# Re-timing two kinds of background DMA around the first down projection of a Macaron layer

## The chip, the cores and the metric

One Trainium2 chip, one of its cores. The metric is device time of one launch in microseconds (us), lower is better; a kernel's time is the median of several runs. A profile is one more execution, recorded by the hardware profiler.

## The reference

One encoder layer over 512 tokens of width 1024, all float32:

```python
x = x + 0.5 * swiglu_ffn(rmsnorm(x, g1), w_gate1, w_up1, w_down1)
x = x + hybrid_mixer(rmsnorm(x, g2), ...)      # attention heads and pooling heads, one output projection
x = x + 0.5 * swiglu_ffn(rmsnorm(x, g3), w_gate2, w_up2, w_down2)
x = rmsnorm(x, g_final)

def swiglu_ffn(x, w_gate, w_up, w_down):       # 1024 -> 2816 -> 1024
    return (silu(x @ w_gate) * (x @ w_up)) @ w_down
```

Only the first feed-forward block (FFN) is touched by the change: its up projection (w_gate, w_up), its down projection (w_down), and the residual x that the down projection is added to.

## The kernel before, in words

**Products.** The 2816 features are 22 tiles of 128. Every matrix product is made of three matmuls of split parts (a high and a low part of each operand, lines 187 to 189, `mm3`). A weight block is loaded from DRAM into a `raw` buffer by the SP queue, then ScalarE (ACT) casts its high part (L131) and VectorE (DVE) subtracts to get the low part (L132); the pair lies in `parts`, or in a `whi`/`wlo` pair. TensorE (PE) works on the pair.

**Up projection, `ffn_up`.** The first five tiles of `down1.order` are "plain" (`PLAIN[0] = 5`), with full products of 512 tokens: the first two together, then n = 2, 3 and 4. The other 17 tiles are done by a seven-product block scheme (as Strassen's) in half-size products of 256 tokens, in a loop written out by hand. Each of those tiles needs two DMAs of 512 KB from `wA` (`fetch`, L458 and L459), issued two tiles ahead as soon as the buffer of an old tile is free. In each tile ACT runs, in order, a copy of one accumulator (L560), the cast of the next tile's first block (`high11`, L466, which needs the DMA of L459), then the copy of the other accumulator `a` (L560). PE may write to a copied accumulator again two products later.

**Down projection, class `Down`.** Also the seven-product scheme: T1 to T4 are sums of blocks of w_down, B11 to B22 the plain blocks. The 48 steps that make T1 to T4 (four sums, six groups g of two feature tiles, a copying and an adding step each) are DMAs from DRAM to DRAM, issued on POOL's queue (L706: `wsum<-in_wB_dram` and, where a finished sum is copied, `wsum<-wsum`; called "sums" below). An adding step waits for the step that wrote its target, a copy of a sum waits until that sum is complete. `make_sums` issues a share of them each time it is called: it first has POOL copy one element of a tile just computed (`mark`, L704), which ties the share to that point of the program, and then issues the DMAs between two entries of `bounds`. It is called once after each of the three plain tiles n = 2, 3, 4, once in each of the 17 half-size tiles, and then at the head of each product as long as shares are left. Before, `bounds` cuts the 48 steps into 22 nearly equal shares of 2 or 3: 20 in the up projection, 2 in the first two products.

**The order of the products.** `product` is called 42 times; PE takes about 2.7 us for a full one (the sixth group is half as large). Products 1 to 18 are T2, B11 and T1 for g = 0 to 5; the weights of the first six are loaded ahead at the end of the up projection (L733). From 19 on T3 and B22 alternate, then come B21 and T4. The SP queue is in program order (`manual_schedule`), so a DMA put into `down1.then[n]` is issued just behind the weight load (L759) of product n, and everything behind it in the queue waits for it to be issued. A weight load waits until its `raw` buffer is free: there are four, and so SP runs a few products ahead of PE.

**The residual.** The buffers of x (four pairs, 256 KB for each of the eight k) are used for other data during the up projection, so x is loaded again from `xT` (L814). `down1.then[8 + k]` puts one reload behind each of products 8 to 15. x[4] to x[7] are first used on DVE after product 19 (`gain(i, 1, 1, ...)`, L821), x[0] and x[1] after product 25 (`shared(i, 0, 1, ...)`, L879), x[2] and x[3] after the last T3 and B22 product, 30. Small constants follow at product 17, and the loading, filling (DVE, L245) and storing of a table for the attention bias at 18, 20 and 25.

Of the kernel before, what the change touches and what calls it, by code (L numbers as in the profile page):

```python
# [19 lines left out]
KD = D // P  # L20
NT = S // P
FF = 2816
KF = FF // P
KH = KF // 2
# [31 lines left out]
def layer(  # L56
# [31 lines left out]
    nc = tc.nc  # L88
# [12 lines left out]
    def name(what):  # L101
        n_tiles[0] += 1
        return f"{what}_{n_tiles[0]}"

    def temp(dtype=F32):
        return tpool.tile([P, S], dtype, tag="t", name=name("t"))
# [15 lines left out]
    def piece(n=1):  # L122
        for _ in range(min(n, len(todo))):
            what, *args = todo.pop(0)
            what(*args)
# [71 lines left out]
    def residual_tiles():  # L197
        pairs = [xpool.tile([P, 2 * S], F32, tag=f"x{k}", name=name("x")) for k in range(KD // 2)]
        x_pairs[:] = pairs
        return [pairs[k // 2][:, k % 2 * S : (k % 2 + 1) * S] for k in range(KD)]  # L200

    x = residual_tiles()
# [33 lines left out]
    def extended():  # L236

        flat = EXT - REL
        ext, far = temp(), temp()

        def load():
            nc.sync.dma_start(ext[:NH, :REL], rel)

        def fill():
            nc.vector.tensor_copy(far[:NH, :flat], ext[:NH, 0:1].to_broadcast([NH, flat]))  # L245

        def store():
            nc.sync.dma_start(ext_d[:, flat:], ext[:NH, :REL])
            nc.sync.dma_start(ext_d[:, :flat], far[:NH, :flat])

        return load, fill, store
# [31 lines left out]
    class Norm:  # L283


        def __init__(self, which):
            self.which, self.h, self.acc = which, {}, None
# [357 lines left out]
    class Down:  # L645
# [11 lines left out]

        def __init__(self, order, pair, block, by_token, ahead=0):  # L660

            self.order, self.pair, self.block, self.by_token = order, pair, block, by_token

            self.terms = {T1: (B11, B12), T2: (T1, B22), T3: (B12, B22), T4: (T2, B21)}
            self.wsum = {
                (i, g): dram.tile(list(block(B11, g).shape), F32, name=name("wsum"))
                for i in self.terms for g in range(G)
            }

            self.ahead = [(i, g) for g in range(2) for i in (T2, B11, T1)]  # L670
            self.loaded, self.then, self.made = {}, {}, []
            self.steps = sorted(
                (g + at + 2 * (i - T1), at, i, g)
                for i in self.terms for g in range(G) for at in range(2)
            )
            n = len(self.steps)
            self.n_sums, self.bounds = 0, [n // 2 * i // ahead for i in range(ahead)]
            left = KF - 2 if ahead else KF
            self.bounds += [n // 2 * bool(ahead) + (n - n // 2 * bool(ahead)) * i // left for i in range(left + 1)]

        def open(self, gs):

# [134 lines left out]
    def whole(make):  # L817
        return [[(make(), 0, S)] for _ in range(2)]

    def scaled(dst, acc, scale, other, op=ALU.add):  # L820
        nc.vector.scalar_tensor_tensor(dst, acc, scale, other, op0=ALU.mult, op1=op)  # L821

    def halved(acc):
        z = [temp() for _ in range(2)]
        for tt in range(2):
            nc.scalar.activation(z[tt], acc[tt][0][0], AF.Copy, scale=0.5)
        return z
# [18 lines left out]

    KPS = (2, 3, 0, 1)
    order1 = [0, 1, KH, KH + 1] + [f + KH * j for f in range(2, KH) for j in range(2)]
    down1 = Down(order1, lambda f: (f % KH, f // KH), block1, False)
    down2 = Down(list(range(KF)), lambda f: (f // 2, f % 2), block2, True, EARLY)  # L850

    with tc.tile_pool(name="act1", bufs=1, reuse_waits="tile") as apool, ExitStack() as in_order:
        down1.begin(apool)
        ffn_up(n1, wA1, down1, False, in_order, PLAIN[0])
        x[:] = residual_tiles()
        for k in range(KD):
            down1.then[8 + k] = [(nc.sync.dma_start, x[k], xT[k])]
        down1.then[17] = [(constants,)]
        for k, what in zip((18, 20, 25), extended()):
            down1.then[k] = [(what,)]  # L860
        p1, p5, p6 = whole(bank), whole(bank), whole(abank)
        for g in range(G):
            down1.product(p6, g, S2, T2)
            down1.product(p1, g, A11, B11)
            down1.product(p5, g, S1, T1)
        p7 = whole(abank)
        u2 = halved(p6)

        def whole_of(i, d, t):

            return x_pairs[2 * d + i].rearrange("p (a c) -> p a c", a=2)[:, :, t * HT : (t + 1) * HT]

        def gain(i, d, t, acc, scale):
            z = whole_of(i, d, t)
            scaled(z, acc[i][0][0].rearrange("p (a c) -> p a c", a=2), scale, z)

        def shared(i, d, t, op):
            z = whole_of(i, d, t)
            nc.vector.tensor_tensor(z, z, u2[i].rearrange("p (a c) -> p a c", a=2), op=op)  # L879

        down1.product(p7, 0, S3, T3)
        for i in range(2):
            scaled(u2[i], p1[i][0][0], 0.5, u2[i], ALU.subtract)
            gain(i, 1, 1, p5, 0.5)
            todo.append((shared, i, 1, 1, ALU.add))
            todo.append((shared, i, 1, 0, ALU.subtract))
            todo.append((shared, i, 0, 1, ALU.subtract))
        for g in range(G):
            if g + 1 < G:
                down1.product(p7, g + 1, S3, T3)  # L890
            down1.product(p5, g, S4, B22, further=True)
            piece()
        for i in range(2):
            todo.append((gain, i, 1, 0, p5, -0.5))
            todo.append((gain, i, 1, 1, p7, 0.5))
        for g in range(G):
            down1.product(p1, g, A12, B21, further=True)
            piece()
        todo.extend((gain, i, 0, 0, p1, 0.5) for i in range(2))
        todo.extend((n2.add, d) for d in range(KD // 2, KD))  # L900
        ahead = down1.tokens(A22, 0, -1.0)
        for g in range(G):
            now = ahead
            if g + 1 < G:
                ahead = down1.tokens(A22, g + 1, -1.0)
            down1.product(p7, g, now, T4, further=True)
            piece()
        for i in range(2):
            gain(i, 0, 1, p7, -0.5)
        for d in range(KD // 2):  # L910
            n2.add(d)
        rooms[:] = [(wpool, "raw", RAW, 1024)]
        part_rooms[:] = [None]
# [14 lines left out]
    with tc.tile_pool(name="mix", bufs=1, reuse_waits="tile") as mpool:  # L928
# [763 lines left out]
        for ds, chunks in (((0, 1, 2, 3), FOUR), ((4, 5), (0, 1)), ((6, 7), (0, 1))):  # L1692
            units = {d: [] for d in ds}
            for chunk in chunks:
                if len(ds) == 4:
                    part, k0 = chunk
                    i = first_out + FOUR.index(chunk)
                    items = [(part, k, d) for k in ((k0, k0 + 1) if part else (k0 + 1, k0)) for d in ds]
                else:
                    part, k0 = chunk, 0  # L1700
                    i = first_out + ds[0] + part
# [3 lines left out]
                for part, k, d in items:  # L1705
                    n = (d * 2 + k - k0) if len(ds) == 4 else ((d - ds[0]) * 4 + k)
# [40 lines left out]
    with tc.tile_pool(name="act2", bufs=1, reuse_waits="tile") as apool, ExitStack() as in_order:  # L1747
# [134 lines left out]
        with tc.manual_schedule(engines={E.PE, E.DVE, E.Activation, E.Pool}):  # L1882
# [12 lines left out]
            lo, n = p7[1][1][1:]  # L1895
# [99 lines left out]
```

## Time and profile before

| What | us |
|---|---|
| median of 3 runs | 831.91 (831.65 to 832.68) |
| the profiled execution, whole | 833.59 |
| its span, first to last instruction | 831.5 |
| PE busy in the span | 819.8 |
| DVE busy in the span | 715.0 |
| ACT busy in the span | 499.9 |

The stages in the profiled execution: up projection of the first FFN to about 224 us, its down projection to about 331 us, the mixer to about 500 us, then the second FFN. The profile's page gives busy time by engine; further views are the waits (who waited for whom), the timeline of an engine's instructions in order, the busy time of each engine in chosen windows (with DMA share, which is the mean busy share of the core's 16 DMA engines and goes above 1 when transfers overlap on an engine, and GB/s moved), and the time from a DMA's issue to its landing. A number in brackets with an arrow in a timeline row is idle time of the engine before that instruction, and what ended it.

### The profile page before, as it was taken

Reading aid. Unit: us, or ns where it says so; the run is one execution under the profiler, and the core shown is the slowest. Engines: PE = TensorE matmul, PEld = TensorE weight load, DVE = VectorE, ACT = ScalarE, POOL = GpSimd, SP = SyncE. Lnnn points to the kernel's source line nnn. Section 1 sums busy time; section 2 is a strip of 40 time slices with the busy share of each in tenths; the row PEclk is TensorE's granted clock in tenths of the full one; section 3 lists DMA queues with packets and bytes.
Section 4 is the critical chain, followed back from the end, with each engine's and each line's share of the span. In section 5 each row is a group of like instructions: output and inputs, shape, how many; then the busy total and the mean of one; then the engine's idle time right before and its main releaser. Section 6 shows DMA issues by size and latency. Waiting matters only on the chain.

```text
span 831.5 us, 15009 instructions
## 1 busy us (share of the span) xinstructions
PE 819.8 (99%) x5730; PEld 755.6 (91%) x5730; DVE 715.0 (86%) x1123; ACT 499.9 (60%) x854; POOL 147.2 (18%) x234
## 2 busy tenths in 40 slices
PE   9999999999999999999999999999999999999996
PEld 7889999999999999878878888899999999988885
DVE  7899999899987987678699688989999999977896
ACT  8346555666656665549659545465665555756573
POOL 0023212222310000334033063111111011100010
PEclk9999999999999999999999999999999999999998
DMA  8266989879998674999411267255666576859632
GB/s 282 73 203 204 239 221 260 205 198 235 253 303 280 194 225 140 240 308 242 173 52 52 82 156 213 68 108 204 160 181 158 148 206 158 275 195 317 202 115 102
DMA packets 73704, 158.56 MB, mean 191 GB/s; under 512 B 6545, under 2 KB 31649, under 8 KB 73249
## 3 DMA queue, kind: packets, MB, share of 16 engines
q1 hardware_dynamic: 49664, 109.09, 39.0%
q0 software_dynamic: 23680, 48.24, 27.6%
q8 instruction: 45, 0.74, 0.4%
q10 hardware_dynamic: 288, 0.27, 0.1%
q14 instruction: 27, 0.21, 0.1%
HBM read 153.38 MB, written 50.34 MB: 245 GB/s over the span
## 4 chain that ended last, share of the span: by engine, by line
PE 94%; DVE 2%; DMA 2%; ACT 1%; issue 0%; SPq 0%; DVEq 0%; ACTq 0%
PE mm L187 21%; PE mm L189 21%; PE mm L188 21%; PE a L187 9%; PE a L188 9%; PE a L189 9%; DMA raw<-in_wQK_dram 1%; PE a L1588 1%; DMA raw<-in_wA_dram 1%; PE mm L1499 1%; PE mm L1563 1%; PE a L1563 0%; PE mm L1588 0%; DVE t L1332 0%; DVE parts L1109 0%
## 5 line engine op out<-in xcount | busy, mean ns | idle before, releaser
L131 ACT CAST parts<-raw 128x1024 fp32r<-128x1024 f32 (+2 forms) x77 | 74.0, 969 | 63.0 <-PE mm L188 27.2
L560 ACT ACTIVATE t<-mm 128x256 f32<-128x256 f32 x105 | 40.3, 384 | 115.3 <-PE mm L189 112.5
L132 DVE TENSOR_TENSOR parts<-raw,parts 128x1024 fp32r<-128x1024 f32 (+2 forms) x77 | 85.7, 1121 | 20.7 <-ACT parts L131 17.5
L187 PE MATMUL mm<-ha,parts 128*128 128x256 f32 x280 | 77.4, 277 | 0.0
L189 PE MATMUL mm<-ha,parts 128*128 128x256 f32 x280 | 77.4, 277 | 0.0
L188 PE MATMUL mm<-ha,parts 128*128 128x256 f32 x280 | 77.4, 276 | 0.0
L706 POOL DMA_DIRECT2D wsum<-in_wB_dram x72 | 71.5, 1167 | 28.1 <-DMA wsum<-wsum 14.5
L704 POOL COPY mark<-t 128x1 f32<-128x1 f32 x40 | 16.1, 402 | 338.2 <-DVE t L604 249.7
L471 DVE TENSOR_TENSOR parts<-wsum,parts 128x1024 fp32r<-128x1024 f32 x53 | 64.6, 1219 | 5.8 <-PE mm L189 4.0
L466 ACT CAST parts<-wsum 128x1024 fp32r<-128x1024 f32 x53 | 53.9, 1049 | 0.4 <-DVE wsum L496 0.2
L187 PE MATMUL mm<-hhi,parts 128*128 128x512 f32 x136 | 53.3, 396 | 0.6 <-ACT parts L131 0.5
L189 PE MATMUL mm<-hhi,parts 128*128 128x512 f32 x136 | 53.2, 394 | 0.0
L188 PE MATMUL mm<-hlo,parts 128*128 128x512 f32 x136 | 52.9, 390 | 0.0
L187 PEld LDWEIGHTS mm<-ha,parts 128*128 128x128 f32 x280 | 52.6, 188 | 0.1
L188 PEld LDWEIGHTS mm<-ha,parts 128*128 128x128 f32 x280 | 52.6, 188 | 0.1
L189 PEld LDWEIGHTS mm<-ha,parts 128*128 128x128 f32 x280 | 52.6, 188 | 0.0
L132 DVE TENSOR_TENSOR ah<-acts,ah 128x512 fp32r<-128x512 f32 (+1 forms) x72 | 47.2, 663 | 5.1 <-ACT ah L131 5.1
L131 ACT CAST ah<-acts 128x512 fp32r<-128x512 f32 (+1 forms) x72 | 40.9, 580 | 9.9 <-PE mm L188 7.6
L471 DVE TENSOR_TENSOR parts<-raw,parts 128x512 fp32r<-128x512 f32 (+1 forms) x52 | 43.5, 860 | 0.0
L489 DVE TENSOR_TENSOR wsum<-raw 128x1024 f32<-128x1024 f32 x35 | 42.7, 1219 | 0.0
L1109 DVE TENSOR_TENSOR parts<-raw,parts 128x1024 fp32r<-128x1024 f32 x24 | 30.3, 1266 | 12.8 <-ACT parts L1104 12.7
L466 ACT CAST parts<-raw 128x512 fp32r<-128x512 f32 (+1 forms) x52 | 39.3, 755 | 2.0 <-DMA raw<-in_wA_dram 1.4
(340 smaller groups left out, 3050.4 us busy)
## 6 DMA issues: line engine op xcount, KB each, us to landing
raw<-in_wA_dram SPq DMA_DIRECT2D x87, 512.0 KB, 4.9
wsum<-in_wB_dram POOLq DMA_DIRECT2D x60, 512.0 KB, 7.7
raw<-wsum SPq DMA_DIRECT2D x36, 512.0 KB, 4.7
raw<-in_wB_dram SPq DMA_DIRECT2D x30, 512.0 KB, 5.1
wsum<-wsum POOLq DMA_DIRECT2D x20, 512.0 KB, 5.3
x<-in_xT_dram SPq DMA_DIRECT2D x16, 256.0 KB, 9.0
raw<-in_wQK_dram SPq DMA_DIRECT2D x8, 512.0 KB, 5.7
wsum<-in_wB_dram POOLq DMA_DIRECT2D x12, 256.0 KB, 6.2
```

The costliest lines, as they stand in the source:

```text
L131: nc.scalar.copy(hi, src)
L132: nc.vector.tensor_tensor(lo, src, hi.bitcast(F32), op=ALU.subtract)
L187: nc.tensor.matmul(acc, a[0], b[0], start=start, stop=False, **more)
L188: nc.tensor.matmul(acc, a[0], b[1], start=False, stop=False, **more)
L189: nc.tensor.matmul(acc, a[1], b[0], start=False, stop=stop, **more)
L466: nc.scalar.copy(hi, src)
L471: nc.vector.tensor_tensor(lo, src, hi.bitcast(F32), op=ALU.subtract)
L489: nc.vector.tensor_tensor(z, raw[:, : 2 * S], raw[:, S : 3 * S], op=ALU.add)
L560: nc.scalar.activation(dst, src, AF.Copy, scale=scale)
L704: nc.gpsimd.tensor_copy(mark[:, 0:1], after[:, 0:1])
L706: nc.gpsimd.dma_start(self.rows(i, g), self.rows(self.terms[i][at], g), **(dict(accum_op=ALU.add) if at else {}),)
L1109: nc.vector.tensor_tensor(lo, buf["raw", i], hi.bitcast(F32), op=ALU.subtract)
```

## The change

The sums: `Down` takes a list `large` of shares for the first calls of `make_sums`. For the first FFN it is (6, 5, 5), so 16 steps are issued in the three plain tiles, the other 32 in the 17 half-size tiles, and none are left for the products. The second FFN's shares stay as they were. The reloads: x[4] to x[7] are issued behind products 13 to 16, x[0] to x[3] behind products 20 to 23; the constants move from 17 to 24, the bias table's three steps from 18, 20 and 25 to 25, 26 and 28.

```diff
@@ -657,7 +657,7 @@
-        def __init__(self, order, pair, block, by_token, ahead=0):
+        def __init__(self, order, pair, block, by_token, ahead=0, large=()):
             self.order, self.pair, self.block, self.by_token = order, pair, block, by_token
@@ -675,8 +675,12 @@
             )
             n = len(self.steps)
             self.n_sums, self.bounds = 0, [n // 2 * i // ahead for i in range(ahead)]
-            left = KF - 2 if ahead else KF
-            self.bounds += [n // 2 * bool(ahead) + (n - n // 2 * bool(ahead)) * i // left for i in range(left + 1)]
+            done = n // 2 * bool(ahead)
+            for many in large:
+                self.bounds.append(done)
+                done += many
+            left = KF - 2 - len(large)
+            self.bounds += [done + (n - done) * i // left for i in range(left + 1)]
         def open(self, gs):
@@ -846,17 +850,18 @@
     KPS = (2, 3, 0, 1)
     order1 = [0, 1, KH, KH + 1] + [f + KH * j for f in range(2, KH) for j in range(2)]
-    down1 = Down(order1, lambda f: (f % KH, f // KH), block1, False)
+    down1 = Down(order1, lambda f: (f % KH, f // KH), block1, False, 0, (6, 5, 5))
     down2 = Down(list(range(KF)), lambda f: (f // 2, f % 2), block2, True, EARLY)
     with tc.tile_pool(name="act1", bufs=1, reuse_waits="tile") as apool, ExitStack() as in_order:
         down1.begin(apool)
         ffn_up(n1, wA1, down1, False, in_order, PLAIN[0])
         x[:] = residual_tiles()
-        for k in range(KD):
-            down1.then[8 + k] = [(nc.sync.dma_start, x[k], xT[k])]
-        down1.then[17] = [(constants,)]
-        for k, what in zip((18, 20, 25), extended()):
+        for k in range(KD // 2):
+            down1.then[13 + k] = [(nc.sync.dma_start, x[KD // 2 + k], xT[KD // 2 + k])]
+            down1.then[20 + k] = [(nc.sync.dma_start, x[k], xT[k])]
+        down1.then[24] = [(constants,)]
+        for k, what in zip((25, 26, 28), extended()):
             down1.then[k] = [(what,)]
         p1, p5, p6 = whole(bank), whole(bank), whole(abank)
         for g in range(G):
```

PE's instructions stand in the same order before and after; on ACT two casts change places, on DVE the filling of the bias table (L245) stands 17 rows later. The lines of the changed kernel are 4 or 5 higher from here on (L706 becomes L710, L759 L763, L814 L818).

POOL's queue in the plain tiles, before: `mark` rows open a share, `wsum_110` to `wsum_115` are the six groups of T1, `wsum_116` to `wsum_121` those of T2, from 122 on T3, from 128 on T4.

```order
L704 COPY mark_471<-t_463 128x1
L706 DMA wsum_110<-in_wB_dram 512x1x256
L706 DMA wsum_111<-in_wB_dram 512x1x256
L704 COPY mark_570<-t_562 128x1
L706 DMA wsum_110<-in_wB_dram 512x1x256
L706 DMA wsum_112<-in_wB_dram 512x1x256
L704 COPY mark_684<-t_678 128x1
L706 DMA wsum_116<-wsum_110 16x8192
L706 DMA wsum_111<-in_wB_dram 512x1x256
L704 COPY mark_766<-t_697 128x1
L706 DMA wsum_113<-in_wB_dram 512x1x256
L706 DMA wsum_117<-wsum_111 16x8192
```

The same place after the change:

```order
L708 COPY mark_471<-t_463 128x1
L710 DMA wsum_110<-in_wB_dram 512x1x256
L710 DMA wsum_111<-in_wB_dram 512x1x256
L710 DMA wsum_110<-in_wB_dram 512x1x256
L710 DMA wsum_112<-in_wB_dram 512x1x256
L710 DMA wsum_116<-wsum_110 16x8192
L710 DMA wsum_111<-in_wB_dram 512x1x256
L708 COPY mark_574<-t_566 128x1
L710 DMA wsum_113<-in_wB_dram 512x1x256
L710 DMA wsum_117<-wsum_111 16x8192
L710 DMA wsum_112<-in_wB_dram 512x1x256
L710 DMA wsum_116<-in_wB_dram 512x1x256
```

The first share has grown from two to six steps, among them two adding steps and a copy that wait for steps of the same share; the second mark stands behind them.

POOL's queue at the end of the stage, before; `ah` are tokens of the down products, so the last two marks stand in products:

```order
L704 COPY mark_2792<-t_2714 128x1
L706 DMA wsum_130<-in_wB_dram 512x1x256
L706 DMA wsum_132<-wsum_120 16x8192
L704 COPY mark_2868<-ah_2753 128x1
L706 DMA wsum_127<-in_wB_dram 512x1x128
L706 DMA wsum_131<-in_wB_dram 512x1x256
L704 COPY mark_2899<-ah_2772 128x1
L706 DMA wsum_133<-wsum_121 16x4096
L706 DMA wsum_132<-in_wB_dram 512x1x256
L706 DMA wsum_133<-in_wB_dram 512x1x128
```

and after, where the row behind the last of them is the mixer's first mark:

```order
L708 COPY mark_2538<-t_2467 128x1
L710 DMA wsum_132<-wsum_120 16x8192
L710 DMA wsum_127<-in_wB_dram 512x1x128
L708 COPY mark_2665<-t_2592 128x1
L710 DMA wsum_131<-in_wB_dram 512x1x256
L710 DMA wsum_133<-wsum_121 16x4096
L708 COPY mark_2797<-t_2719 128x1
L710 DMA wsum_132<-in_wB_dram 512x1x256
L710 DMA wsum_133<-in_wB_dram 512x1x128
L708 COPY mark_4329<-parts 128x1
```

Three steps fewer are left for the end: the last mark on a `t` tile is followed by the two last steps, and the two marks on `ah` are gone.

SP's queue from product 7 on, before; `raw` rows are the weights of products 7, 8, and so on, `x` rows the reloads (two rows a pair of k):

```order
L759 DMA raw_3052<-wsum_118 128x1024
L759 DMA raw_3085<-in_wB_dram 128x4x256
L814 DMA x_2854<-in_xT_dram 128x512
L759 DMA raw_3118<-wsum_112 128x1024
L814 DMA x_2854<-in_xT_dram 128x512
L759 DMA raw_3152<-wsum_119 128x1024
L814 DMA x_2855<-in_xT_dram 128x512
L759 DMA raw_3188<-in_wB_dram 128x4x256
L814 DMA x_2855<-in_xT_dram 128x512
L759 DMA raw_3221<-wsum_113 128x1024
L814 DMA x_2856<-in_xT_dram 128x512
L759 DMA raw_3256<-wsum_120 128x1024
```

The same after:

```order
L763 DMA raw_3042<-wsum_118 128x1024
L763 DMA raw_3075<-in_wB_dram 128x4x256
L763 DMA raw_3107<-wsum_112 128x1024
L763 DMA raw_3140<-wsum_119 128x1024
L763 DMA raw_3175<-in_wB_dram 128x4x256
L763 DMA raw_3207<-wsum_113 128x1024
L763 DMA raw_3241<-wsum_120 128x1024
L818 DMA x_2861<-in_xT_dram 128x512
L763 DMA raw_3275<-in_wB_dram 128x4x256
L818 DMA x_2861<-in_xT_dram 128x512
L763 DMA raw_3310<-wsum_114 128x1024
L818 DMA x_2862<-in_xT_dram 128x512
```

Between the weights of products 8 and 13 nothing is left; the reloads begin behind product 13, with the pair that holds x[4] and x[5].

## Prediction

> **What bounds the kernel now.** I read the page first, then the waits of PE, then the timelines around the one wait that lies in the changed stage, then the windows for the DMA engines.
>
> ```profile
> span 831.5 us, 15009 instructions
> PE 819.8 (99%) x5730; PEld 755.6 (91%) x5730; DVE 715.0 (86%) x1123; ACT 499.9 (60%) x854; POOL 147.2 (18%) x234
> ```
>
> PE is busy for 99% of the span. Whatever a DMA does counts only where PE runs dry, and the busy row leaves 831.5 - 819.8 = 11.7 us for that in the whole program. The waits of PE name the places (us in total, times, longest):
>
> ```profile
> ...
> PE mm L189 <- DVE parts L132: 0.8, 1, 0.8
> PE mm L1499 <- DVE sm L1507: 0.7, 2, 0.5
> PE a L1342 <- DVE t L1332: 0.6, 1, 0.6
> ...
> ```
>
> The two left out lie at the start of the program, the two with lines above 1300 in the mixer. Only that on L132 is in the first down projection. PE's timeline there:
>
> ```profile
> 250.81 0.28 PE L189 MATMUL a<-ah,wlo 128*128 128x256 f32 x1
> ...
> 251.50 0.28 PE L189 MATMUL a<-ah,wlo 128*128 128x256 f32 x1
> 251.83 0.38 PE L187 MATMUL mm<-ah,parts 128*128 128x256 f32 x1
> 252.05 0.28 PE L188 MATMUL mm<-ah,parts 128*128 128x256 f32 x1
> 253.09 0.39 PE L189 MATMUL mm<-ah,parts 128*128 128x256 f32 x1 [0.76 <-DVE parts L132]
> 253.31 0.28 PE L187 MATMUL mm<-ah,parts 128*128 128x256 f32 x1
> ```
>
> Six undisturbed starts take 251.50 - 250.81 = 0.69 us, 0.115 each. The four from 251.50 to 253.31 take 1.81 instead of 0.46. So the stall costs 1.35 us, more than the 0.76 in brackets, because the matmuls on both sides of it are stretched too. It is the only place from 66 to 330 us where I find the starts off their step.
>
> What was late? ACT's timeline, with the cast ahead of that split, and SP's:
>
> ```profile
> 250.72 1.05 ACT L131 CAST parts<-raw 128x1024 fp32r<-128x1024 f32 x1 [3.67 <-DMA raw<-in_wB_dram]
> 236.31 0.38 SPq L759 DMA_DIRECT2D raw<-in_wB_dram  x1
> ```
>
> The cast waited 3.67 us for a load. Counting weight loads and casts in queue order, it is product 11's B11, issued at 236.31: 14 us for 512 KB. The windows (last two columns: DMA share and GB/s) and the landing times of all `raw` loads from 230 to 262 us say why:
>
> ```profile
> 225.00:245.00 20.00, 20.00 (x179) 20.00 (x178) 17.34 (x23) 12.77 (x19) 4.95 (x6) 1.00 1.14 296
> 245.00:255.00 10.00, 9.18 (x78) 8.79 (x77) 5.23 (x7) 4.98 (x7) 0.00 (x0) 1.00 1.13 336
> 265.00:275.00 10.00, 10.00 (x90) 10.00 (x89) 8.18 (x12) 7.19 (x10) 0.00 (x0) 1.00 0.66 223
> DMA to landing us min/median/max: 3.3/10.2/13.7
> ```
>
> At 296 to 336 GB/s the engines are oversubscribed, and loads queue behind each other until PE has used up its lead.
>
> **The change part by part.**
>
> *Sums taken out of 213 to 245 us.* POOL's timeline has these late sums before:
>
> ```profile
> 222.84 1.16 POOL L706 DMA_DIRECT2D wsum<-in_wB_dram  x1
> ...
> 232.10 1.15 POOL L706 DMA_DIRECT2D wsum<-in_wB_dram  x1 [4.44 <-DMA wsum<-wsum]
> 243.31 1.14 POOL L706 DMA_DIRECT2D wsum<-in_wB_dram  x1 [10.06 <-DMA wsum<-wsum]
> ```
>
> With the four rows left out these are seven steps, four of 512 KB and three of 256 KB (the half-size group), 2.75 MB. Afterwards two are left there, 0.75 MB. So 2.0 MB leave.
>
> *Reloads taken out of 228 to 254 us.* Eight of 256 KB:
>
> ```profile
> L814 SPq DMA_DIRECT2D x<-in_xT_dram x8: 378/461/751, 228.8 to 253.4; - x8
> ```
>
> The six behind products 8 to 13 fall into 225 to 245: 1.5 MB. Of the 296 GB/s x 20 us = 5.9 MB moved there, 3.5 MB go. The load of product 11 then finds engines under half full and should land within the 5.8 us that was the longest from 262 to 300 us:
>
> ```profile
> DMA to landing us min/median/max: 3.1/4.6/5.8
> ```
>
> The load was 14 us late against about 5, the stall 1.35 us: it goes with a wide margin. **Term: -1.35 us.** Next late would be the same row of loads further on, below.
>
> *Reloads put behind products 13 to 16 and 20 to 23.* x[4] to x[7] are first needed by DVE at 270.97, x[0] and x[1] at 280.25:
>
> ```profile
> 270.97 1.26 DVE L821 SCALAR_TENSOR_TENSOR x<-mm,x 128x512 f32<-128x512 f32 x2
> ...
> 280.25 0.67 DVE L879 TENSOR_TENSOR x<-x,t 128x512 f32<-128x512 f32 x1
> 280.85 1.21 DVE L132 TENSOR_TENSOR parts<-raw,parts 128x1024 fp32r<-128x1024 f32 x1
> 262.33 0.82 SPq L759 DMA_DIRECT2D raw<-wsum  x2
> ```
>
> The second weight load at 262.33 is product 20's. x[0] and x[1] are thus issued by about 265 and have 15 us, x[4] to x[7] more. Each reload holds SP for 0.46 us (median above) ahead of the next weight load, and 1 MB over the 11 us of products 20 to 23 adds 95 GB/s to the 223 of the window 265:275: 318, for a short time in the range of 296 to 336. What hides it: the split at 280.85 is product 25's, ready at 282. PE begins product 11 at 251.5; from there to product 25 are 11 full products and three half ones, 12.5 x 2.75 us (24 starts of 0.115) and the stall, so it begins product 25 at 287.2. Loads may slip by some 5 us. **Term: 0**, up to +1.4 if that lead is gone.
>
> *Constants and the bias table.* Four small DMAs move down the same queue; their issue time is paid on SP, which waits for free buffers anyway. DVE's fill (L245) now stands behind product 25's split, one product after its load is issued, so DVE may wait there by 1 or 2 us, inside the same 5 us of lead; the store at 28 holds SP as long. **Term: 0.**
>
> *Sums put into 41 to 95 us.* This is the part with two answers. Sixteen steps instead of six are issued by the third plain mark. Windows:
>
> ```profile
> 40.00:66.00 26.00, 26.00 (x131) 22.14 (x130) 25.73 (x35) 14.58 (x21) 6.01 (x7) 1.00 0.56 162
> 66.00:95.00 29.00, 29.00 (x258) 29.00 (x258) 27.36 (x39) 16.79 (x30) 8.76 (x13) 1.00 0.94 265
> ```
>
> 26 x 162 + 29 x 265 GB/s is 11.9 MB; ten more steps of 0.52 MB make 17.1 MB in 55 us, 311 GB/s. That is full. Who waits? The `fetch` of each half-size tile:
>
> ```profile
> 67.14 0.55 SPq L459 DMA_DIRECT2D raw<-in_wA_dram  x1
> 75.92 0.55 SPq L459 DMA_DIRECT2D raw<-in_wA_dram  x1
> 84.90 0.33 SPq L458 DMA_DIRECT2D raw<-in_wA_dram  x1
> 94.42 0.33 SPq L458 DMA_DIRECT2D raw<-in_wA_dram  x1
> 74.42 0.62 ACT L466 CAST parts<-raw 128x512 fp32r<-128x512 f32 x1 [0.33 <-DMA raw<-in_wA_dram]
> 75.01 0.39 ACT L560 ACTIVATE t<-a 128x256 f32<-128x256 f32 x1
> 83.45 0.61 ACT L466 CAST parts<-raw 128x512 fp32r<-128x512 f32 x1
> 84.59 0.38 ACT L560 ACTIVATE t<-a 128x256 f32<-128x256 f32 x1 [0.52 <-PE a L189]
> ```
>
> The tile period is 94.42 - 84.90 = 9.52 us. The copy of `a` at 84.59 began as PE ended; a period earlier that is 75.07. PE returns to `a` one half-size product (12 x 0.115 = 1.38 us) later, so the copy of 0.39 must begin by 76.06 and the cast in front of it by 75.47: the load of 67.14, which landed 7.2 us after issue, may take 8.3. The next, issued at 75.92 for the cast at 83.45, may take 9.0. From 160 to 190 us, with POOL's sums beside them, such loads landed like this, and PE did not stall:
>
> ```profile
> DMA to landing us min/median/max: 3.6/5.7/8.0
> ```
>
> A tile's fetch is 1.05 MB per 9.52 us, 110 GB/s, under half of 311; unlike SP's own pile at 230 us it cannot queue behind itself. I take 0, by this row; the other end is a landing of 9 to 9.5 us in the first three or four tiles, 0.5 to 1 us of stall in each. [...]
>
> POOL itself falls behind, since copies in the big shares wait for steps of the same share. Its marks hold temporary tiles; the tightest is the second half-size tile's mark, behind the copy that waits for the 14th step. Its buffer is next written by the copy of `a` three tiles after 75.01's, at 75.07 + 3 x 9.52 = 103.6. Fourteen steps and six fetches are 13.6 MB; at 296 GB/s from 41 us on that is done at 87. **Term: 0**, 16 us of room.
>
> **Sum.** 831.5 - 1.35 = 830.15 us of span. The profiled execution took 833.59 in all, 1.68 above the median of 831.91; I take the difference to the median: 831.91 - 1.35 = 830.56, so **830.6 us**. About 0.2% (1.66 us) is what a measurement of this kernel can tell from no change.
>
> **The rivals.**
>
> *Starved fetches in the first half-size tiles (slower).* For it: the 311 GB/s and the cast at 74.42, which already waited 0.33 us. Against it: 8.0 us landings without a stall. It decides from landings of 8.3 us in the first tile and 9.0 later. Three or four tiles at 0.5 to 1 us give 1.5 to 4, with the gain -1.35 a time of 832.1 to 834.6; as a case that ends slower I price it at +3.1 - 1.35, 833.6. Chance 0.13.
>
> *The stall moves to products 20 to 26.* Reloads, constants and the late fill all meet there, and DVE was busy throughout from 275 to 285, so what is late there is not caught up soon:
>
> ```profile
> 275.00:285.00 10.00, 10.00 (x91) 10.00 (x90) 10.00 (x14) 6.04 (x9) 0.00 (x0) 1.00 0.82 268
> ```
>
> The lead of 5 us speaks against it. It would give back the gain: 831.9. Chance 0.14.
>
> *More than the one stall goes.* The runs timed without a profile may lose more at product 11 than the profiled one; another 0.5 to 1 us gives 829.8. Nothing in the profile shows it. Chance 0.11.
>
> That the change does nothing at all (the loads late for another reason) I count with the second rival.
>
> **How the numbers follow.** Forecast 0.62; it covers 830.0 to 831.2. The range reaches from the gain case, 829.8, to most of the slower case, 833.2. Faster by over 0.2% (below 830.25): the gain case and 0.07 of the forecast, 0.18. Slower (above 833.57): about half of the first rival and a little for what I overlook, 0.09. Within: 0.73.
>
> **What would show it.** Right: no wait of PE on DVE parts L132 near 252 us, DMA share from 225 to 245 well under 1, the `raw` loads there landing in about 5 us, the window 40:66 near 300 GB/s. Wrong: waits of ACT's L466 on DMA over 1 us with a wait of PE behind them from 66 to 110 us, or a new wait of PE between 270 and 300 us.

## The result and the profile after

The changed kernel takes 838.49 us (median of 4 runs, 837.9 to 839.57), the kernel before on the same chip 832.29 (831.65 to 833.48): a ratio of 1.0073, 95% interval 1.0061 to 1.0085. It is slower by 6.2 us, where 830.6 was forecast. The profiled execution took 838.52 us with a span of 836.4, 4.9 us more than that of before. Ratios in this document are of executions near full clock; one of e14 below, 1180.18 us at a mean clock of 0.654, is in none of them.

From the page after: span, busy times, and the clock granted to PE in 40 slices of the span.

```profile
span 836.4 us, 15008 instructions
PE 822.6 (98%) x5730; PEld 759.0 (91%) x5730; DVE 715.2 (86%) x1123; ACT 499.8 (60%) x854; POOL 146.3 (17%) x232
PEclk9998999999999999999999999999999999999999
```

PE is busy 2.8 us longer with the same 5730 matmuls, so some of them ran slower: the fourth slice (63 to 84 us) has a clock under 0.9. The waits of PE after (total, times, longest):

```profile
PE a L187 <- ACT t L560: 3.1, 1, 3.1
...
```

The wait on L132 at product 11 is gone, as forecast. New, and the longest after the start of the program, is one wait for ACT's copy of an accumulator (L560). PE's timeline at that place:

```profile
75.73 0.28 PE L189 MATMUL mm<-xa,parts 128*128 128x256 f32 x1
79.09 0.58 PE L187 MATMUL a<-ha,parts 128*128 128x256 f32 x1 [3.08 <-ACT t L560]
79.47 0.41 PE L188 MATMUL a<-ha,parts 128*128 128x256 f32 x1
...
85.01 0.36 PE L187 MATMUL mm<-ha,parts 128*128 128x256 f32 x1
85.21 0.28 PE L188 MATMUL mm<-ha,parts 128*128 128x256 f32 x1
85.32 0.28 PE L189 MATMUL mm<-ha,parts 128*128 128x256 f32 x1
```

PE stands still from 75.73 to 79.09: 3.36 us from start to start instead of 0.11, a loss of 3.25. Then the starts are 0.21 apart instead of 0.11 until 85.21: 28 steps in 6.12 us that take 3.18 at the full rate, a loss of 2.94. 3.25 + 2.94 - 1.35 (the stall that went) = 4.84, and the spans differ by 4.9. So this one place is the whole difference of the two profiled executions. The medians differ by 6.2, as much as 3.25 + 2.94 alone: the profiled execution of before was 1.3 us above its median, so the timed runs need not have had the whole old stall.

What ACT and SP did there, and how long the two halves of that fetch took from issue to landing:

```profile
66.88 0.55 SPq L459 DMA_DIRECT2D raw<-in_wA_dram  x1
78.13 0.62 ACT L466 CAST parts<-raw 128x512 fp32r<-128x512 f32 x1 [4.36 <-DMA raw<-in_wA_dram]
78.66 0.38 ACT L560 ACTIVATE t<-a 128x256 f32<-128x256 f32 x1
DMA to landing us min/median/max: 6.9/9.0/11.2
```

It is the fetch that the prediction followed (issued at 67.14 before, cast at 74.42). It lands after 11.2 us instead of 7.2; the cast waits for it, the copy of `a` stands behind the cast on ACT, and PE needs that copy. POOL's timeline shows what was in flight beside it, and the windows how the DMA engines were used (last three columns: clock, DMA share, GB/s):

```profile
62.01 0.50 POOL L710 DMA_DIRECT2D wsum<-wsum  x1 [6.32 <-DMA wsum<-in_wB_dram]
62.50 3.21 POOL L710 DMA_DIRECT2D wsum<-in_wB_dram  x3
...
70.78 0.52 POOL L710 DMA_DIRECT2D wsum<-wsum  x1 [4.26 <-DMA wsum<-in_wB_dram]
71.28 3.90 POOL L710 DMA_DIRECT2D wsum<-in_wB_dram  x4
```

```profile
40.00:66.00 26.00, 26.00 (x133) 22.18 (x132) 25.73 (x34) 14.58 (x21) 11.38 (x14) 1.00 0.87 245
65.00:70.00 5.00, 5.00 (x46) 5.00 (x46) 4.93 (x7) 1.73 (x5) 1.52 (x2) 1.00 1.02 134
...
80.00:85.00 5.00, 5.00 (x25) 5.00 (x25) 3.12 (x5) 0.39 (x2) 0.00 (x0) 0.50 1.13 257
225.00:245.00 20.00, 20.00 (x178) 20.00 (x178) 19.35 (x28) 15.33 (x23) 3.26 (x3) 1.00 1.04 280
245.00:255.00 10.00, 10.00 (x91) 10.00 (x90) 9.58 (x13) 7.16 (x11) 0.00 (x0) 1.00 0.84 258
```

Four steps were given to the queue from 62.01 to 65.5, just ahead of the fetch. From 65 to 70 us the DMA share is 1.02, and only 134 GB/s are moved (before: 0.47 and 138). The clock of 0.50 from 80 to 85 is the slow stretch of PE.

### The profile page after: what moved, and what is told of

Its sections match the earlier page's. It is cut to its first block, busy times and chain, and to the rows that moved or that the text cites. A ratio compares the mean times of both kernels' runs of the same rounds, so it can differ in the third digit from the quotient of the medians.

```text
span 836.4 us, 15008 instructions
## 1 busy us (share of the span) xinstructions
PE 822.6 (98%) x5730; PEld 759.0 (91%) x5730; DVE 715.2 (86%) x1123; ACT 499.8 (60%) x854; POOL 146.3 (17%) x232
## 3 DMA queue, kind: packets, MB, share of 16 engines
q0 software_dynamic: 23680, 48.24, 27.6%
HBM read 153.38 MB, written 50.34 MB: 244 GB/s over the span
## 4 chain that ended last, share of the span: by engine, by line
PE 91%; DVE 3%; DMA 3%; ACT 1%; issue 1%; DVEq 0%; SPq 0%; ACTq 0%
PE mm L187 21%; PE mm L188 20%; PE mm L189 20%; PE a L187 9%; PE a L188 9%; PE a L189 9%; DMA raw<-in_wA_dram 1%; DMA raw<-in_wQK_dram 1%; PE a L1593 1%; PE mm L1568 1%; PE mm L1504 1%; PE a L1568 0%; PE mm L1593 0%; DVE t L1337 0%; DMA gain_sb<-in_gains_dram 0%
## 5 line engine op out<-in xcount | busy, mean ns | idle before, releaser
L560 ACT ACTIVATE t<-mm 128x256 f32<-128x256 f32 x105 | 40.3, 384 | 116.7 <-PE mm L189 113.9
L132 DVE TENSOR_TENSOR parts<-raw,parts 128x1024 fp32r<-128x1024 f32 (+2 forms) x77 | 85.7, 1121 | 17.1 <-ACT parts L131 16.6
L710 POOL DMA_DIRECT2D wsum<-in_wB_dram x72 | 71.3, 1176 | 16.2 <-DMA wsum<-in_wB_dram 7.9
L132 DVE TENSOR_TENSOR ah<-acts,ah 128x512 fp32r<-128x512 f32 (+1 forms) x72 | 47.2, 662 | 6.3 <-ACT ah L131 6.3
L187 PE MATMUL a<-ha,parts 128*128 128x256 f32 x140 | 39.5, 282 | 3.1 <-ACT t L560 3.1
```

The source lines that it names most:

```text
L132: nc.vector.tensor_tensor(lo, src, hi.bitcast(F32), op=ALU.subtract)
L187: nc.tensor.matmul(acc, a[0], b[0], start=start, stop=False, **more)
L560: nc.scalar.activation(dst, src, AF.Copy, scale=scale)
L710: nc.gpsimd.dma_start(self.rows(i, g), self.rows(self.terms[i][at], g), **(dict(accum_op=ALU.add) if at else {}),)
```

## The experiments

The theory after the result: (1) the early sums alone cost the time, through the one late fetch; (2) what makes it late are steps still in flight when it is issued, the adding ones above all; (3) the late cast costs because the copy that PE needs stands behind it; (4) the half clock follows the stall and is no second effect of the transfers. The rivals are named with each run. The kernel before took 832.16 to 832.65 us on the chips of these runs.

**One half of the change at a time.** First the sums alone (reloads, constants and bias table as before), then the reloads, constants and table alone (shares as before).

```diff
 e1: down1 = Down(..., 0, (6, 5, 5))      +for k in range(KD): down1.then[8 + k] = ...   (as before)
 e2: -down1 = Down(..., 0, (6, 5, 5))     +down1 = Down(order1, ..., False)              (as before)
```

> Sums in shares of 6, 5 and 5, reloads and constants where they were. My theory now: the changed kernel loses in the up projection alone, because the big shares make the fetch issued at 66.9 us land 11.2 us later, PE stands still for 3.3 us and then runs at half the clock for 6 us (2.9 us more); and it gains the 1.35 us of product 11 either way, since the sums alone take 2.0 of 5.9 MB out of 225 to 245 us. So: the same loss, about 838.4 us, no PE wait near 252 us. Rival, that the late reloads or the late bias table cost something too: then this kernel is faster than the changed one by that cost, under 837. Rival, that product 11's stall needs the reloads gone: 839.8 and a PE wait there.

> Reloads, constants and bias table late, sums in 22 nearly equal shares as before. My theory: nothing happens in the up projection; taking 1.5 MB of reloads out of 225 to 245 us is enough for product 11's load to land in time, so 1.35 us go: 830.9 us. Rival, that the late sums and not the reloads made that load late: 832.2, with a PE wait near 252 us. Rival, that the late reloads and the late table stall PE between 270 and 300 us: above 832.5 with a wait there.

e1 took 836.15 us (835.49 to 840.18), ratio 1.0054 (1.003 to 1.0078); e2 831.84 (830.9 to 832.86), ratio 0.9989 (0.998 to 0.9999). PE's timeline of e1:

```profile
75.99 0.28 PE L189 MATMUL mm<-xa,parts 128*128 128x256 f32 x1
79.40 0.39 PE L187 MATMUL a<-ha,parts 128*128 128x256 f32 x1 [3.13 <-ACT t L560]
79.62 0.28 PE L188 MATMUL a<-ha,parts 128*128 128x256 f32 x1
79.74 0.28 PE L189 MATMUL a<-ha,parts 128*128 128x256 f32 x1
```

The same stall, 3.41 us, but here the starts are 0.11 to 0.12 apart from the second on: no half clock in this execution. (The run of 840.18 had a mean clock of 0.993, the others 0.997 and 0.998.) So the sums carry the loss. The size was missed: e1 is 2.3 us below the changed kernel, under the 837 at which the late reloads were to share the blame. e2 speaks against that, as it has the late reloads and is no slower than before; that the half clock, seldom in e1, is the difference is argued from the clocks of the runs. Neither e1 nor e2 has a wait of PE near 252 us: in their profiles either half alone removes the old stall. For e2, the windows and the landings of the `raw` loads from 230 to 262 us:

```profile
225.00:245.00 20.00, 20.00 (x179) 20.00 (x178) 18.48 (x25) 14.91 (x21) 4.98 (x6) 1.00 1.15 291
245.00:255.00 10.00, 10.00 (x91) 10.00 (x90) 7.13 (x11) 5.08 (x7) 0.00 (x0) 1.00 1.11 348
DMA to landing us min/median/max: 2.9/5.8/10.2
```

The engines are as full as before (1.14 and 1.13), yet the longest landing is 10.2 us instead of 13.7, and that was enough.

**Other shares.** With the late reloads, `large` = (2, 2, 2), (6, 5, 1) and (6, 3, 3):

```diff
-    down1 = Down(order1, ..., False, 0, (6, 5, 5))
+    down1 = Down(order1, ..., False, 0, (2, 2, 2))      # e3;  e4: (6, 5, 1);  e8: (6, 3, 3)
```

> The changed kernel with shares of 2, 2 and 2 in the plain tiles, so as many as before there, and 42 steps over the 17 half-size tiles, none in the products. My theory: the big shares are what costs; without them the fetch at 66.9 us lands in about 7 us, no stall, and product 11's stall stays away: 830.9 us. If 2.5 steps a tile are too many for the fetches beside them, small waits of ACT's L466 on DMA come up later in the up projection, each under 1 us: up to 832.

> The changed kernel with only the third share cut from 5 to 1; the 4 steps go to the half-size tiles. My theory counts the bytes of sums in flight beside the fetch of 66.9 us: the three steps of the second share issued at 62.5 us are still there, the four at 71.3 us are not, so the fetch lands after 8 to 9.5 us instead of 11.2, PE stalls by 0 to 1.3 us, too short for the clock to drop: 831 to 832.3 us. Rival, that the steps already in the queue when the fetch is issued decide alone: it still lands after about 11 us and the kernel stays at 838.

> The changed kernel with shares of 6, 3 and 3 in place of 6, 5 and 5 (36 steps are left for the 17 tiles behind). Theory A (what lies in the steps' queue when the first half-size tile's fetch is issued, near 66.9 us, decides: with a second share of 3 that queue has run out by about 62 us): the landing is 7 to 8.5 us, no PE gap over 1 us near 76 us, later tiles carry 2.1 steps each and none of them stalls; the time is 831.3 to 832.5 us. Theory B (any concentration of steps ahead of the half-size tiles makes a fetch late): a PE gap of 1 to 3 us near 76 us or at the next tile near 85 to 95 us, 833.5 us or more.

Landing and gap (from PE's last start ahead of the stall to the first behind it) are of the one profiled execution, the time is the median.

| | us | ratio to before (95%) | landing of the fetch near 67 us | PE's gap near 76 us |
|---|---|---|---|---|
| e3 (2, 2, 2) | 833.8 | 1.0017 (1.0008 to 1.0027) | 6.8 | none |
| e4 (6, 5, 1) | 837.26 | 1.005 (1.0034 to 1.0066) | 10.4 | 2.55 |
| e8 (6, 3, 3) | 833.89 | 1.0024 (1.0012 to 1.0035) | 11.1 | 3.23 |
| after (6, 5, 5) | 838.49 | 1.0073 (1.0061 to 1.0085) | 11.2 | 3.36 |

All three were slower than expected, e3 by stalls in later tiles (below). The executions scatter, e4 from 833.77 to 838.72 us and e8 from 832.87 to 836.87, with mean clocks from 0.994 to 0.998; e8's profiled one took 835.92, so its gap is not that of the median. In e8 the six steps of the first share were not through by 62 us. Its POOL timeline:

```profile
63.60 0.50 POOL L710 DMA_DIRECT2D wsum<-wsum  x1 [5.88 <-DMA wsum<-in_wB_dram]
64.09 1.23 POOL L710 DMA_DIRECT2D wsum<-in_wB_dram  x1
...
66.42 1.95 POOL L710 DMA_DIRECT2D wsum<-in_wB_dram  x2
```

Again four steps in the 4 us around the fetch. The third share, which e4 cuts to one step, matters little to the landing.

**The second share taken away.** Shares of 6 and 0.

> The changed kernel with shares of 6 and 0 ahead (42 steps left for the 18 tiles behind, 2.33 each). Theory A (steps of the second share that are still queued at 66 us make the fetch late): the six run out by 63 us, nothing of the sums lies beside the first half of the fetch, and it lands in 4 to 7 us; no PE gap over 0.5 us near 76 us; 831.5 to 833 us. Theory B (the first share alone is enough): a landing over 9 us, a gap of 1 us or more, 834 us or more.

The fetch near 67 us lands after 7.2 us and PE has no gap there: steps of the second share are what it met. The time was missed all the same, 836.27 us (833.75 to 839.66), ratio 1.0049 (1.0026 to 1.0072), because two later tiles stall. POOL, then PE, in e13:

```profile
108.16 3.12 POOL L710 DMA_DIRECT2D wsum<-in_wB_dram  x3 [0.30 <-issue]
139.43 3.54 POOL L710 DMA_DIRECT2D wsum<-in_wB_dram  x3 [0.24 <-issue]
```

```profile
123.77 0.28 PE L189 MATMUL mm<-xa,parts 128*128 128x256 f32 x1
125.21 0.38 PE L187 MATMUL a<-ha,parts 128*128 128x256 f32 x1 [1.16 <-ACT t L560]
...
153.76 0.28 PE L189 MATMUL mm<-xa,parts 128*128 128x256 f32 x1
155.83 0.43 PE L187 MATMUL a<-ha,parts 128*128 128x256 f32 x1 [1.79 <-ACT t L560]
156.05 0.41 PE L188 MATMUL a<-ha,parts 128*128 128x256 f32 x1
```

Each stall follows, one tile later, on three steps from `in_wB_dram` issued together; the fetches behind them, issued at 113.95 and 143.94, landed after 10.2 and 10.9 us. e3 has the same pair twice (three steps at 165.15 and 185.93, gaps of 1.25 at 180.76 and 1.39 at 201.11). A third such row in e13, at 170.38, has no gap behind it. In the kernel before no half-size tile from 89 to 215 us issues more than two such steps at a time, and none stalls. Four of five is a strong hint, not an experiment of its own. Three such steps at once are not needed either: e1 has a further gap of 0.93 us at 107.96, e14 of 0.92 and 0.66 at 95.44 and 105.88, and e15 of 0.89 at 104.74, each behind four or more steps that POOL issued within 4 to 7 us.

**Adding or number?** e7 makes every adding step of the first block a plain copy over its target. e14 and e15 go back to equal shares and put five extra steps into the second plain tile's share, on the memory of a sum that is made later: copies in e14, one copy and four additions in e15.

```diff
 e7:  -   **(dict(accum_op=ALU.add) if at else {}),
      +   **(dict(accum_op=ALU.add) if at and self is not down1 else {}),
 e14: +   if self is down1 and at == 1:
      +       part = part + [(0, 0, T3, G - 2) for j in range(5)]               # e15: int(j > 0) for the second 0
```

> The changed kernel with 6, 5, 5, but each step that adds a block of weights to a sum is a plain copy over it (the sums then hold only their last term, which leaves out the additions of the first down product's weight sums). Number, order, sizes of what is written and dependencies of the steps stay. Theory A (the adding steps load the DMA engines with the extra reading of what they add to, so the fetch queued beside them is late): the fetch of 66.9 us lands in 7 to 9 us instead of 11.2, the PE gap is under 1 us and the time is 831.5 to 833.5 us. Theory B (the number of steps and their rows beside the fetch decides, adding or not): it lands in 10 us or more, the gap is 2 to 3.3 us and the time 835 to 838.5 us.

> Equal shares and late reloads (fetch of 66.9 us lands in 6.3 us, no gap), with five extra steps behind the second plain tile's own: plain copies of a block of weights into the memory of a sum that is made, and so overwritten, later; the output is the same. Theory A (adding is what costs): the five are through or thin when the fetch is issued, landing 6 to 8 us, gap under 0.6 us, 831.5 to 833 us. Theory B (the number of steps decides): landing over 9.5 us, gap of 1.5 us or more, 834 us or more.

> As e14_five_more_copies, but four of the five extra steps add to what the first of them copied (the sum's memory is overwritten later; the output is the same). Theory A (adding is what costs): landing 10 to 12 us, a gap of 2 to 3.5 us, 834.5 to 838 us, against no gap with copies. Theory B (number): landing and gap within 1 us of those with five copies.

e7 took 833.48 us (832.6 to 839.9), ratio 1.003 (1.0009 to 1.0051): its landing is still 10.0 us and the gap 2.12. Its quicker steps brought the next share forward; five steps of it were issued from 66.61 to 68.94, on top of the fetch. So number alone can do it too. What an addition costs is in the pages, POOL's DMA queue (packets, MB, share of the 16 engines' span), after and in e7:

```profile
q0 software_dynamic: 23680, 48.24, 27.6%
```

```profile
q0 software_dynamic: 14208, 48.24, 22.2%
65.00:70.00 5.00, 5.00 (x45) 5.00 (x45) 4.93 (x7) 1.67 (x5) 4.43 (x6) 1.00 1.07 378
```

The same bytes take 9472 packets less, and 0.276 x 836.4 - 0.222 x 831.4 = 46 us of the engines' time less, 1.9 us for each of the 24 adding steps. A copying step takes about 1.4 us by these shares (an estimate: 0.222 x 831.4 = 185 us, less 46 for the 24 additions of the second FFN, over the 96 steps of both), an adding one so a little over twice as much. From 65 to 70 us a like share (1.07) moves 378 GB/s instead of 134. The pages count the same bytes with and without additions (153.38 MB read from HBM in both), so if an addition reads its target, that is not in the GB/s.

In e14 and e15 the extra steps waited for one another, as they have one target, so that only one lay beside the fetch; the pair does not tell number from adding at full size. For one step it does. Landing of the extra step issued ahead of the fetch (a copy in e14, an addition in e15), and the window, in e14 and then in e15:

```profile
DMA to landing us min/median/max: 4.2/4.2/4.2
65.00:70.00 5.00, 5.00 (x45) 5.00 (x45) 4.96 (x7) 1.68 (x6) 0.82 (x2) 1.00 0.67 177
```

```profile
DMA to landing us min/median/max: 6.5/6.5/6.5
65.00:70.00 5.00, 5.00 (x45) 5.00 (x44) 4.93 (x7) 1.68 (x6) 1.17 (x1) 1.00 0.64 81
```

A share of 0.64 to 0.67 moves 177 GB/s with a copy and 81 with an addition, and the fetch lands after 5.4 and 6.9 us. The times are 833.26 us (ratio 1.0007, 0.9997 to 1.0017) and 834.07 (1.003, 1.0019 to 1.0041).

**The copy that PE waits for, ahead of the cast.** e5 moves the cast and the work on the same load behind both accumulator copies in all half-size tiles, e9 only in the second and third of the first block.

```diff
-                high11(n + 1)
-                low11(n + 1)
...
                 last_sums()
-                sum13(n + 1)
                 copy(z[:, HT:], up_hi, -1.0)
                 product(acc, cut(w24, 0, S), S2, False)
                 copy(u[:, HT:], acc, -1.0)
-                sum24(n + 1)
+                high11(n + 1)
+                low11(n + 1)
+                sum13(n + 1)
...
+                sum24(n + 1)
                 high13(n + 1)
```

> The changed kernel, with the first half-size tile's cast of freshly fetched weights (and the vector engine's difference and sum that read the same block) put behind the two accumulator copies in each half-size tile's order, so that a fetch that lands late holds ScalarE only after PE's copies are out; the 6, 5, 5 sums and the late reloads stay. Theory A (the late landing costs only because ScalarE, held at that cast, cannot copy the accumulator): the fetch issued near 66.9 us still lands about 11 us later, but the PE gap near 76 to 79 us is under 0.6 us, no stretch of PE at half clock follows, and the time falls from 838.5 to 831 to 833 us. Theory B (the transfers of the steps slow PE by themselves, or the weights are needed by PE itself soon after): a gap of 2 to 3 us stays, moved by one or two products, and the time stays above 836 us.

> The changed kernel (6, 5, 5 and late reloads) with the order of e5_cast_behind_copies only in the second and third half-size tile, where the late fetches of 66.9 and 75.7 us are cast; every other tile keeps the changed kernel's order. Theory A (late cast holds the copy that PE waits for; the 4 us that e5 still lost were the new order's own cost in the other tiles of both up projections): no PE gap over 0.7 us at 75 to 80 us, PE at full clock, landings still 9 to 11 us, time 831.5 to 833.5 us. Theory B (the early sums cost PE time in some other way, which e5 showed): 835 us or more, as e5.

e5 took 836.63 us (836.3 to 837.4), ratio 1.0053 (1.0037 to 1.0069); e9 835.79 (834.94 to 836.4), 1.0037 (1.0023 to 1.0051). Landings of 10.3 and 11.5 us, no gap near 76 us, clock 1.00 throughout: the mechanism of the stall is right. The times are not what I expected of it. PE's timeline of e9:

```profile
83.00 0.28 PE L188 MATMUL a<-xa,whi 128*128 128x256 f32 x1
84.29 0.38 PE L189 MATMUL a<-xa,wlo 128*128 128x256 f32 x1 [1.01 <-DVE wlo L471]
...
85.45 0.28 PE L189 MATMUL a<-xa,wlo 128*128 128x256 f32 x1
86.09 0.39 PE L187 MATMUL mm<-xa,parts 128*128 128x256 f32 x1 [0.37 <-ACT t L560]
...
97.09 0.28 PE L189 MATMUL mm<-xa,parts 128*128 128x256 f32 x1
98.28 0.38 PE L187 MATMUL a<-ha,parts 128*128 128x256 f32 x1 [0.92 <-ACT t L560]
```

These three gaps (1.29, 0.64, 1.19) cost 2.8 us. The late load delays DVE's sums and with them the next tile's weights; a better order on ACT saves the clock and passes the lateness on. Part of e5's loss is its order's own: against e2, the same PE row is 0.33 us late at 27 us, 2.47 at 350 (350.07 against 347.60) and the span 3.8 (834.2 against 830.4), so 1.3 us are lost behind that row, where no fetch of the second FFN took over 6.7 us to land (6.8 in e2).

**Idle time without transfers.** e2 with eight, six or four copies of 128x512 on ACT ahead of the cast in the first half-size tile.

```diff
+                if n == plain and not loaded:
+                    for _ in range(8):                   # e10: 6;  e11: 4
+                        nc.scalar.copy(sg, norm.rb)
                 high11(n + 1)
```

> Equal shares of the sums and late reloads (the kernel without the stall, 831.8 us), plus eight copies of 128x512 on ScalarE (about 0.53 us each, 4.2 us; they write a tile that is overwritten later, the output is unchanged) ahead of the cast of fetched weights in the first half-size tile. No transfer is added or moved. Theory A (the idle of PE by itself brings the half clock, in some executions): a PE gap of 2.8 to 3.3 us at 76 to 79 us; in some executions PE runs at half rate for some 6 us behind it: runs between 835 and 838.5 us, mean clock 0.994 to 0.997. Theory B (the half clock comes from the burst of transfers beside PE): the same gap, never a half clock, every run within 834.5 to 835.5 us at 0.997 or 0.998.

> As e6_scalar_delay, with six copies in place of eight, 0.64 us each: 3.9 us, of which 0.8 us is slack, ahead of the cast in the first half-size tile; no transfer added. A PE gap of 3.1 us at 66 to 70 us. Theory A (half clock follows an idle of PE of roughly 3 us, if it falls badly, transfers or none): some executions lose 3.1 us and some up to 3 us more, 834.5 to 838 us, and the profiled one shows whether its clock fell. Theory B (the half clock needs the longer idle of e6, over 4 us, or transfers): all executions lose 3.1 us and nothing else, 834.5 to 835.5 us.

> As e6_scalar_delay, with four copies: 2.6 us, of which 0.8 us is slack. A PE gap of 1.8 us at 66 to 69 us. Theory A (a gap of under 2 us is too short for the clock to fall): 833.3 to 834.2 us, no run over 835 us, clock 0.996 to 0.998. Theory B (any pause may bring it): some runs at 835.5 to 837 us with 0.995 or less.

| | PE's gap | us | ratio to before (95%) | mean clock of the runs |
|---|---|---|---|---|
| e6, 8 copies | 4.47 | 838.03 (837.75 to 838.12) | 1.0068 (1.005 to 1.0086) | 0.996 in four of 4 |
| e10, 6 copies | 3.18 | 836.26 (835.99 to 838.26) | 1.0049 (1.0033 to 1.0064) | 0.994 to 0.996 in four of 4 |
| e11, 4 copies | 1.86 | 833.65 (833.11 to 836.13) | 1.0016 (1.0006 to 1.0025) | 0.996 to 0.998 in nine of 10, 0.995 in that of 836.13 |

In e6 the gap came at 66 us, not 76 (the first tile's cast stands there), and was larger than expected, as the copies took 0.64 us each instead of 0.53. PE's timeline and two windows of e6:

```profile
66.17 0.28 PE L189 MATMUL mm<-xa,parts 128*128 128x256 f32 x1
70.64 0.39 PE L187 MATMUL a<-ha,parts 128*128 128x256 f32 x1 [4.19 <-ACT t L560]
70.87 0.28 PE L188 MATMUL a<-ha,parts 128*128 128x256 f32 x1
...
71.44 0.41 PE L187 MATMUL a<-ha,parts 128*128 128x256 f32 x1
...
73.14 0.41 PE L189 MATMUL mm<-ha,wlo 128*128 128x256 f32 x1
```

```profile
65.00:70.00 5.00, 1.45 (x12) 1.25 (x11) 2.00 (x3) 4.78 (x9) 2.71 (x3) 1.00 0.61 210
70.00:75.00 5.00, 4.36 (x24) 4.36 (x25) 3.55 (x5) 0.86 (x3) 0.60 (x2) 0.66 0.93 210
```

From 71.44 to 73.14 eight starts take 1.70 us, 0.21 each. The half rate comes with no added transfer, at a DMA share of 0.61 and 0.93, and 0.8 us after PE has started again. So it follows the pause.

**The better half again.** e2 in five rounds.

> The kernel of e2_reloads_only again (equal shares, late reloads), for a closer comparison. Theory A (the late reloads take the 1.35 us stall at product 11 away and cost nothing): 831.0 to 831.9 us, ratio 0.998 to 0.9995. Theory B (the gain of e2 was scatter): ratio within 0.9995 to 1.001.

831.99 us (831.47 to 834.38), ratio 0.9994 (0.9985 to 1.0003): below before by 0.35 us here, by 0.8 in e2. The sign holds in both, the size is under what this measurement can tell. It is the only version with a median below that of before.

## Why the prediction was wrong, point by point

- **The stall at product 11, -1.35 us:** right in the profile, where it went; the medians of e2 and e12 show only 0.81 and 0.35 of it. Its working was not: I said 3.5 of 5.9 MB leave the stretch from 225 to 245 us and the load then finds the engines under half full. They stayed at a share of 1.04 (1.14 before), and in the same stretch of the program, which comes 6.1 us later now (231.2 to 251.2), at 0.93 and 247 GB/s, about 1 MB less than before. Landings were up to 7.6 us, and e2 shows that a little less lateness suffices. One slip is in the sum: some of the seven steps counted from 213 us on had been issued before 225.
- **Reloads, constants and table later, 0:** right. PE has no wait from 250 to 330 us, and from 262 to 300 us the weight loads land within 5.5 us (5.8 before). The rival that moved the stall to products 20 to 26 did not come.
- **POOL behind its marks, 0:** right. A mark came as late as 86.99 us, and nobody waited for it.
- **The sums put into 41 to 95 us, 0: the step that failed.** "Unlike SP's own pile at 230 us it cannot queue behind itself. I take 0, by this row": the row was 8.0 us, of fetches beside two steps of the sums at a time. With four the fetch took 11.2, and ACT held the copy that PE needed. The stretch from 40 to 66 us, where I looked for about 300 GB/s, moved 245 at a share of 0.87. The tolerance worked out just ahead of it, 8.3 us, was right: 11.2 - 8.3 = 2.9, and PE waited 3.08. The wrong turn was to measure room in GB/s: I called 311 GB/s full and compared it with 296 to 336 elsewhere, while the engines had a share of 1.02 at 134 with additions among the steps. Copies alone can fill them too: in e7 they had a share of 1.07 at 378, and the fetch was late all the same.
- **A longer backlog on POOL's row.** The term of 0 also needs that more steps beside the fetch take no more from it than two do. That was my assumption, and no run shows it. In the runs the fetch landed after 6.3 to 7.2 us with two steps issued beside it (before, e2, e3, e13), and after 10.3 to 11.5 with four (after, e1, e4, e5, e8, e9).
- **The slower rival** was the right mechanism (chance 0.13), mis-sized: several stalls of 0.5 to 1 us were priced, +3.1 in all. It was one of 3.25, after which PE's own lateness gave the next fetches room (9.4 us for the one of 75.67, no gap), and then 2.94 us at half clock, for which the sum had no term. The stall alone would have brought the forecast to 830.6 + 3.25 = 833.8, a little past the range's end of 833.2; the half clock put it far past.

What stays open: which of number and adding weighs more in the changed kernel itself, why four steps (and mostly three in later tiles) are the point at which the fetch tips from 7 to over 10 us, and how much of the 1.35 us the timed runs of before had.

## What to carry to other kernels

Price background transfers by the time they hold the DMA engines, not by their bytes: read the DMA share beside the GB/s (1.02 at 134 GB/s in the changed kernel, 1.07 at 378 in e7), and treat an adding DMA as about twice a copy (3.4 us of the engines' time against 1.4 here, by the estimate above). Spread them so that few are in flight when a load with little slack is issued; an even spread of 2.2 a tile (48 steps in 22 shares) was free, most bursts of three or four were not. And six of the eight gaps of PE of 2 us or more told of here cost 1.7 to 2.94 us again in clock, while none of up to 1.86 us did: one long stall can be worse than the same time in short ones.

## What the runs showed of the hardware

- **Half clock of PE followed six of the eight gaps of 2 us or more told of here.** It came behind gaps of 4.47, 3.36, 3.23, 3.18, 2.55 and 2.07 us (e6, after, e8, e10, e4, e13) and not behind gaps of 3.41, 2.12 and 1.86 in the profiled executions of e1, e7 and e11. It set in at once or up to 0.8 us after PE had started again, lasted 3.4 to 3.6 us and cost 1.7 each time (a clock of 0.66 over 5 us, from 70 to 75 us in e6 and from 155 to 160 in e13) but in the changed kernel, where it lasted 6.1 and cost 2.94. Why a gap of 2.07 us had it and one of 3.41 had not, these runs do not show.
- **The adding DMAs moved smaller packets than the copies.** 24 adding steps as copies: 9472 packets less for the same bytes (12288 fewer of under 2 KB), 1.9 us of the engines' time less for each (27.6% of 836.4 us against 22.2% of 831.4). POOL, too, was longer at issuing one: 1.18 us against 0.70 (the second of the extra steps, at 64.99 in e15 and 64.41 in e14).
